# Low parts of every fourth weight piece made by an accumulating DMA instead of VectorE, in a two-layer float32 encoder trunk

## The chip, the cores and the metric

The kernel runs on one core of one Trainium2 chip. The metric is device time in microseconds (us) from the start to the end of the program. The kernel before was timed twice: 2804.89 and 2805.33 us, median 2805.11 us.

## The reference

Two layers of a bidirectional encoder on 256 tokens of width 2048, all in float32. Each layer projects the input, runs two kinds of attention, merges them through gates, and ends in a SwiGLU block; both halves are closed by a residual and a layer norm.

```python
def hybrid_layer(x, rel_bias, w_in, sink, w_pa, w_pb, w_out, ln1_g, ln1_b, w_up, w_down, ln2_g, ln2_b):
    proj = jnp.einsum('bsd,dc->bsc', x, w_in)
    qa, ka, va, qb, kb, vb, ga, gb = jnp.split(proj, split_points, axis=-1)
    ya = dilated_mixture(qa, ka, va, rel_bias).astype(dt) @ w_pa
    yb = windowed_gqa(qb, kb, vb, rel_bias, sink).astype(dt) @ w_pb
    merged = jax.nn.sigmoid(ga) * ya + jax.nn.sigmoid(gb) * yb
    x = layer_norm(DEEPNORM_ALPHA * x + merged @ w_out, ln1_g, ln1_b)
    gate, up = jnp.split(x @ w_up, 2, axis=-1)
    x = layer_norm(DEEPNORM_ALPHA * x + (jax.nn.silu(gate) * up) @ w_down, ln2_g, ln2_b)
    return x
```

The weights are 503 MB in all (w_in 2048 x 10240, w_up 2048 x 11264 and w_down 5632 x 2048 in each layer are the large ones), and every weight is used once. So the kernel streams weights from DRAM and multiplies them with activations that stay on the chip.

## The kernel before

**Two parts for every weight.** A float32 product is made of products in the chip's faster float32r format. A weight is split in a high part, the value rounded to float32r, and a low part, the value minus its high part. Activations are split in the same way. A product of tiles is then three matmuls: high by high, high by low, low by high.

**Pieces.** The weights come in 960 pieces of 512 KB, each a tile `raw` of 128 partitions by 1024 float32. `piece` (line 110) appends a piece to a list when the products are declared, and `run` (line 137) walks the list: piece `m` gets its matmuls, then, where it is the last of its product, the evacuation of the accumulator (`post`), then one step of a list of background work (attention).

Each product over the model width in `gemm_w` (line 157) has four pieces; a piece of it has eight high matmuls of 512 columns (line 202) and eight low ones of 256 columns (line 171), alternating. `gemm_a` (line 219) turns the product round, with 2 or 4 k tiles in a piece and three matmuls for each (lines 215 to 217, of which 216 reads the low part).

The order of the list in each layer, numbered from 0 in layer 0: values of attention A, pieces 0 to 23; values of B 24 to 27; keys and queries of B 28 to 47; queries and keys of A 48 to 95; then the gates and merges, 96 to 183; w_out 184 to 215; w_up, first half, 216 to 311; w_down 312 to 359; w_up, second half, 360 to 439; w_down 440 to 479. Layer 1 is the same from 480 on. In the gates and merges a cycle of eleven pieces comes back: four of a gate for A, four of a gate for B, one of w_pa, two of w_pb; four cycles are 44 pieces. Everywhere else in `gemm_w` the products start at a piece number that 4 divides.

**Loading and splitting.** `split_to` (line 121) makes the two parts of a piece. It runs ahead of the matmuls: before piece `m` is multiplied, pieces up to `m + 3` have been issued to the splitting engines, and up to eight or nine ahead close to a layer norm. The high part is a copy on ScalarE (ACT) into a tile `whi` (line 128), the low part a subtraction on VectorE (DVE) into a tile `wlo` (line 129). `load_to` (line 114) issues the loads from SyncE's DMA queue (SPq, line 118), five pieces ahead of the split, into six buffers: the load of piece `s + 6` must wait until piece `s` has been read by both splitting instructions.

The parts live in a pool of 38 buffers of 512 KB (`units`) which they share with the activations.

**What sets the order.** All engines run in program order; nothing is rescheduled. So on ACT the evacuation of a product (line 281, `tmp<-acc`) stands between the copies of the pieces three ahead of the product's last one and those that come after. ACT reaches the evacuation early, waits there for the last matmul of the product, and then copies the next pieces in one burst. The GpSimd engine (POOL) does nothing but eight tiny power operations in the layer norms (`rstd`, line 401).

Of the kernel before, what the change touches and what calls it, by code (L numbers as in the profile page):

```python
# [10 lines left out]
F32 = mybir.dt.float32  # L11
F32R = mybir.dt.float32r
BF16 = mybir.dt.bfloat16
AF = mybir.ActivationFunctionType
ALU = mybir.AluOpType
# [61 lines left out]
def trunk(ctx: ExitStack, tc: tile.TileContext, x, rel_bias, w_in, sink, w_pa, w_pb, w_out,  # L77
          ln1_g, ln1_b, w_up, w_down, ln2_g, ln2_b, hot, mask, eye, out):
    nc = tc.nc
    x = x[0]  # L80
    out = out[0]
# [10 lines left out]
    def unit(shape, dt, name):  # L92
        return units.tile(shape, dt, name=name, tag="u")
# [13 lines left out]
    state = {"load": 0, "split": 0}  # L107
# [6 lines left out]
    def load_to(m):  # L114
        while state["load"] < min(m, len(pieces)):
            pc = pieces[state["load"]]
            pc["raw"] = work.tile([P, pc["kk"], pc["cc"]], F32, name="raw", tag="raw", bufs=N_RAW)
            nc.sync.dma_start(pc["raw"], pc["src"])  # L118
            state["load"] += 1

    def split_to(m):
        while state["split"] < min(m, len(pieces)):
            load_to(state["split"] + 1 + AHEAD_LOAD)
            pc = pieces[state["split"]]
            raw = pc["raw"]
            hi = unit([P, pc["kk"], pc["cc"]], F32R, "whi")
            lo = unit([P, pc["kk"], pc["cc"]], F32R, "wlo")
            nc.scalar.activation(hi, raw, AF.Copy)  # L128
            nc.vector.tensor_tensor(out=lo, in0=raw, in1=hi.bitcast(F32), op=ALU.subtract)  # L129
            pc["hi"], pc["lo"] = hi, lo  # L130
            state["split"] += 1

# [4 lines left out]
    def run():  # L137

        for m, pc in enumerate(pieces):
            ahead = min(AHEAD_SPLIT, 1 + m)  # L140
            for n in norms:
                if n - 24 <= m < n:
                    ahead = max(ahead, min(n - m + AHEAD_NORM, AHEAD_SPLIT + (m - n + 24) // 3))
            split_to(m + 1 + ahead)
            if pc["pre"]:
                pc["pre"]()
            pc["mm"](pc)
            if pc["post"]:
                pc["post"]()
            if background:  # L150
                background.pop(0)()
            pieces[m] = None
# [662 lines left out]
    for c in range(1, 4):  # L815
        load_to(2 * c - 1)
        load_x(c)
    make(0)
    split_to(1)
    make(1)  # L820
    run()
# [28 lines left out]
```

## Time and profile before

| what | value |
|---|---|
| time, median of 2 runs | 2805.11 us |
| profiled execution | 2805.18 us, span 2803.4 us from the first instruction to the last |
| PE busy | 2778.0 us, 99% of the span |
| DVE, ACT, POOL busy | 1591.9 us (57%), 1263.2 us (45%), 5.4 us (0%) |
| granted TensorE clock, mean | 0.997 |
| DMA | 532.07 MB, mean 190 GB/s |

The page lists each engine's busy time, the chain of work that ended last, and groups of instructions with what ended the idle time before them. TensorE (PE) works nearly without a gap. The other engines wait most of their idle time for it, which costs nothing. In the timeline, a row is a stretch of like instructions with its start, its length, their count, and in brackets the idle time of the engine before it and what ended that.

### The profile page before, as it was taken

How to read it: one execution, taken by the hardware profiler on the slowest of the kernel's cores; microseconds unless marked ns; L12 is line 12 of the kernel's file. 1: busy time of each engine (PE TensorE's matmuls, PEld its weight loads, DVE VectorE, ACT ScalarE, POOL GpSimd, SP SyncE). 2: the span in 40 equal slices, each digit the busy share in tenths (PEclk: the TensorE clock that was granted, in tenths of full speed). 3: DMA queues.
4: the chain of work that ended last, by engine and by line, in shares of the span. 5: the costliest groups of instructions: out<-in, count | busy, mean ns of one | idle time of the engine just before them, and what ended most of it. 6: DMA issues, size and time to landing. Idle time of an engine off the chain costs nothing.

```text
span 2803.4 us, 38529 instructions
## 1 busy us (share of the span) xinstructions
PE 2778.0 (99%) x15467; PEld 2409.8 (86%) x15467; DVE 1591.9 (57%) x1886; ACT 1263.2 (45%) x1600; POOL 5.4 (0%) x13
## 2 busy tenths in 40 slices
PE   9999999999999999999999999999999999999998
PEld 7888888889888888888888888888888888888887
DVE  4466555576655544555566655566665555455555
ACT  4354444454444443444444545444544444334451
POOL 0000000000000000000000000000000000000000
PEclk9999999999999999999999999999999999999999
DMA  8766656664655555555746665655746556556564
GB/s 236 228 181 182 184 171 193 196 208 151 212 191 185 190 202 179 180 189 190 243 143 203 182 188 166 195 186 180 237 151 194 183 188 229 180 168 192 182 210 143
DMA packets 494982, 532.07 MB, mean 190 GB/s; under 512 B 52288, under 2 KB 424000, under 8 KB 494804
## 3 DMA queue, kind: packets, MB, share of 16 engines
q1 hardware_dynamic: 493524, 527.53, 59.6%
q8 instruction: 121, 1.98, 0.3%
q10 hardware_dynamic: 1280, 2.10, 0.3%
q14 instruction: 57, 0.47, 0.1%
HBM read 522.86 MB, written 6.68 MB: 189 GB/s over the span
## 4 chain that ended last, share of the span: by engine, by line
PE 97%; DVE 1%; SPq 1%; DMA 1%; ACT 0%; issue 0%; DVEq 0%; POOL 0%; ACTq 0%; POOLq 0%
PE acc L202 44%; PE acc L171 22%; PE acc L216 9%; PE acc L217 9%; PE acc L215 9%; SPq L118 1%; PE aux L297 0%; PE aux L296 0%; PE aux L295 0%; DMA res<-in_x_dram 0%; DMA raw<-in_w_in_dram 0%; DVE xT L392 0%; PE aux L551 0%; PE aux L517 0%; PE aux L609 0%; PE aux L533 0%
## 5 line engine op out<-in xcount | busy, mean ns | idle before, releaser
L202 PE MATMUL acc<-xT,whi 128*128 128x512 f32 x4880 | 1719.5, 398 | 0.0
L171 PE MATMUL acc<-xT,wlo 128*128 128x256 f32 x4928 | 1357.1, 281 | 0.0
L129 DVE TENSOR_TENSOR wlo<-raw,whi 128x1024 fp32r<-128x1024 f32 x960 | 1126.7, 1220 | 242.6 <-ACT whi L128 235.3
L128 ACT ACTIVATE whi<-raw 128x1024 fp32r<-128x1024 f32 x960 | 965.4, 1050 | 331.1 <-DMA raw<-in_w_down_dram 129.1
L202 PEld LDWEIGHTS acc<-xT,whi 128*128 128x128 f32 x4880 | 908.8, 188 | 206.1 <-DVE xT L392 0.3
L171 PEld LDWEIGHTS acc<-xT,wlo 128*128 128x128 f32 x4928 | 931.0, 189 | 13.4
L281 ACT ACTIVATE tmp<-acc 128x512 f32<-128x512 f32 x186 | 110.9, 596 | 745.0 <-PE acc L202 744.7
L215 PE MATMUL acc<-whi,hT 128*128 128x512 f32 (+1 forms) x784 | 288.1, 367 | 0.0
L217 PE MATMUL acc<-whi,hT 128*128 128x512 f32 (+1 forms) x784 | 288.1, 367 | 0.0
L216 PE MATMUL acc<-wlo,hT 128*128 128x512 f32 (+1 forms) x784 | 288.1, 367 | 0.0
L667 DVE TENSOR_TENSOR sg<-acc,tmp 128x512 f32<-128x512 f32 x76 | 52.5, 691 | 242.5 <-ACT tmp L281 242.5
L215 PEld LDWEIGHTS acc<-whi,hT 128*128 128x128 f32 x784 | 147.9, 189 | 24.4
L216 PEld LDWEIGHTS acc<-wlo,hT 128*128 128x128 f32 x784 | 147.8, 189 | 24.4
L217 PEld LDWEIGHTS acc<-whi,hT 128*128 128x128 f32 x784 | 147.8, 189 | 24.2
L754 DVE TENSOR_TENSOR tmp<-acc,tmp 128x512 f32<-128x512 f32 x44 | 30.4, 691 | 178.5 <-ACT tmp L281 178.5
L215 PE MATMUL acc<-whi,mT 128*128 128x512 f32 (+1 forms) x320 | 111.1, 347 | 0.0
L216 PE MATMUL acc<-wlo,mT 128*128 128x512 f32 (+1 forms) x320 | 110.9, 347 | 0.0
L217 PE MATMUL acc<-whi,mT 128*128 128x512 f32 (+1 forms) x320 | 110.9, 347 | 0.0
L435 DVE SCALAR_TENSOR_TENSOR res<-res,acc 128x1024 f32<-128x1024 f32 (+2 forms) x20 | 20.2, 1008 | 156.7 <-PE acc L217 156.7
L215 PE MATMUL acc<-whi,xT 128*128 128x512 f32 (+1 forms) x256 | 95.8, 374 | 2.9 <-ACT whi L128 2.9
L216 PE MATMUL acc<-wlo,xT 128*128 128x512 f32 (+1 forms) x256 | 95.0, 371 | 3.1 <-DVE wlo L129 3.1
L217 PE MATMUL acc<-whi,xT 128*128 128x512 f32 (+1 forms) x256 | 94.4, 369 | 0.0
(137 smaller groups left out, 1626.1 us busy)
## 6 DMA issues: line engine op xcount, KB each, us to landing
raw<-in_w_up_dram SPq DMA_DIRECT2D x352, 512.0 KB, 3.8
raw<-in_w_in_dram SPq DMA_DIRECT2D x320, 512.0 KB, 4.9
raw<-in_w_down_dram SPq DMA_DIRECT2D x176, 512.0 KB, 6.0
raw<-in_w_out_dram SPq DMA_DIRECT2D x64, 512.0 KB, 5.8
raw<-in_w_pb_dram SPq DMA_DIRECT2D x32, 512.0 KB, 3.9
raw<-in_w_pa_dram SPq DMA_DIRECT2D x16, 512.0 KB, 4.8
bias<-ftab SPq DMA_DIRECT2D x96, 64.0 KB, 3.7
ftab<-fb SPq DMA_DIRECT2D x7, 640.0 KB
```

Source lines behind the costliest of these rows:

```text
L118: nc.sync.dma_start(pc["raw"], pc["src"])
L128: nc.scalar.activation(hi, raw, AF.Copy)
L129: nc.vector.tensor_tensor(out=lo, in0=raw, in1=hi.bitcast(F32), op=ALU.subtract)
L171: nc.tensor.matmul(st["acc"][:, n, 0:SEQ], lhsT=lo[:, k, n * P:(n + 1) * P], rhs=xs(4 * j + k)[:, 0, :], start=False, stop=False)
L202: nc.tensor.matmul(acc, lhsT=hi[:, k, n * P:(n + 1) * P], rhs=xs(kt).rearrange("p h t -> p (h t)"), start=first and not turn, stop=last)
L215: nc.tensor.matmul(o, lhsT=xk[:, 0, ts], rhs=hi, start=first, stop=False)
L216: nc.tensor.matmul(o, lhsT=xk[:, 0, ts], rhs=lo, start=False, stop=False)
L217: nc.tensor.matmul(o, lhsT=xk[:, 1, ts], rhs=hi, start=False, stop=last)
L281: nc.scalar.activation(tmp, acc[:, :, SEQ:2 * SEQ], AF.Copy, scale=scale)
L435: nc.vector.scalar_tensor_tensor(r, r, scale, acc, op0=ALU.mult, op1=ALU.add)
L667: nc.vector.tensor_tensor(out=dst, in0=acc[:, :, 0:SEQ], in1=tmp, op=ALU.add)
L754: nc.vector.tensor_tensor(out=tmp, in0=acc[:, :, 0:SEQ], in1=tmp, op=ALU.add)
```

## The change

For pieces 10, 14, 18 and so on to 958, 238 in all, VectorE's subtraction goes. ACT writes the negated high part into the low tile with a second copy of the raw piece at a scale of -1, and a DMA on GpSimd's queue then adds the raw piece to it in place: -high + raw is the low part.

```diff
             nc.scalar.activation(hi, raw, AF.Copy)
-            nc.vector.tensor_tensor(out=lo, in0=raw, in1=hi.bitcast(F32), op=ALU.subtract)
+            if state["split"] % 4 == 2 and state["split"] > 8:
+                nc.scalar.activation(lo, raw, AF.Copy, scale=-1.0)
+                nc.gpsimd.dma_start(lo, raw, accum_op=ALU.add)
+            else:
+                nc.vector.tensor_tensor(out=lo, in0=raw, in1=hi.bitcast(F32), op=ALU.subtract)
```

In the changed kernel lines from 130 on stand four lower in the file: 281 becomes 285, 290 becomes 294, and so on; the new copy is line 130, the accumulating DMA line 131, the subtraction line 133.

On ACT, at the end of the first merge in layer 0 (`mT` is the split of the merged activations, `sg` a gate, `tmp` an evacuated accumulator), before:

```order
L290 ACTIVATE mT<-sg 128x2x256
L128 ACTIVATE whi<-raw 128x1024 x4
L281 ACTIVATE tmp<-acc 128x512
L711 ACTIVATE sg<-sg 128x512
L128 ACTIVATE whi<-raw 128x1024 x4
```

and in the changed kernel:

```order
L294 ACTIVATE mT<-sg 128x2x256
L128 ACTIVATE whi<-raw 128x1024
L130 ACTIVATE wlo<-raw 128x1024
L128 ACTIVATE whi<-raw 128x1024 x3
L285 ACTIVATE tmp<-acc 128x512
L715 ACTIVATE sg<-sg 128x512
```

Pieces 118 to 121 are copied here; 118 gets its second copy at once, and the other three stand one copy later.

On SPq, the loads of pieces 113 to 117 (the two of w_pb in the first merge and the three behind them) go into the buffers that pieces 107 to 111 held; the names in brackets are the semaphores waited for (DMAHW are SPq's own transfers, DMASW the GpSimd queue's, Activation and DVE the engines). Before:

```order
L118 DMA raw<-in_w_pb_dram 128x4x256 [waits DMAHW2_49,DVE_49]
L118 DMA raw<-in_w_pb_dram 128x4x256 [waits DMAHW3_49,DVE_49]
L118 DMA raw<-in_w_in_dram 128x4x256 [waits DMAHW4_49,DVE_49]
L118 DMA raw<-in_w_in_dram 128x4x256 [waits DMAHW5_49,DVE_49]
L118 DMA raw<-in_w_in_dram 128x4x256 [waits DMAHW6_49,DVE_49]
```

and in the changed kernel:

```order
L118 DMA raw<-in_w_pb_dram 128x4x256 [waits DMAHW2_49,DVE_49]
L118 DMA raw<-in_w_pb_dram 128x4x256 [waits DMAHW3_49,DVE_49]
L118 DMA raw<-in_w_in_dram 128x4x256 [waits DMAHW4_49,DVE_49]
L118 DMA raw<-in_w_in_dram 128x4x256 [waits DMAHW5_49,DMASW1_49,Activation_49]
L118 DMA raw<-in_w_in_dram 128x4x256 [waits DMAHW6_49,DVE_49]
```

The load of piece 116 now waits for the accumulating DMA of piece 110 to land, as one load in four does, and the loads behind it on the queue wait with it.

On POOL, from the start of the kernel to the first layer norms, in the changed kernel (before, only the `minus_half` row and the L401 rows stand there):

```order
L815 MEMSET minus_half 128x1
L131 DMA wlo<-raw 128x1024 x53
L405 ISA
L405 TENSOR_TENSOR rstd<-rstd,minus_half 128x1 x2
L131 DMA wlo<-raw 128x1024 x66
```

POOL issues the 238 DMAs in order (53, 66, 54 and 65), and the power operations of the norms stand between them.

## Rows read from the trace of the kernel before

**Rows 1.** The page: busy time and share of each engine; clock in 40 slices.

```profile
PE 2778.0 (99%) x15467; PEld 2409.8 (86%) x15467; DVE 1591.9 (57%) x1886; ACT 1263.2 (45%) x1600; POOL 5.4 (0%) x13
...
PEclk9999999999999999999999999999999999999999
```

**Rows 2.** The page: the chain that ended last, by engine.

```profile
PE 97%; DVE 1%; SPq 1%; DMA 1%; ACT 0%; issue 0%; DVEq 0%; POOL 0%; ACTq 0%; POOLq 0%
```

**Rows 3.** The page's costliest groups: busy us, mean ns | idle before, releaser.

```profile
L202 PE MATMUL acc<-xT,whi 128*128 128x512 f32 x4880 | 1719.5, 398 | 0.0
L171 PE MATMUL acc<-xT,wlo 128*128 128x256 f32 x4928 | 1357.1, 281 | 0.0
L129 DVE TENSOR_TENSOR wlo<-raw,whi 128x1024 fp32r<-128x1024 f32 x960 | 1126.7, 1220 | 242.6 <-ACT whi L128 235.3
L128 ACT ACTIVATE whi<-raw 128x1024 fp32r<-128x1024 f32 x960 | 965.4, 1050 | 331.1 <-DMA raw<-in_w_down_dram 129.1
```

**Rows 4.** Waits of PE: us in total, times, longest us.

```profile
PE aux L370 <- DMA res<-in_x_dram: 4.6, 2, 3.1
PE acc L216 <- DVE wlo L129: 3.1, 4, 0.9
PE acc L215 <- ACT whi L128: 2.9, 2, 2.8
```

**Rows 5.** Timeline of ACT, gates and merges of layer 0, 380 to 432 us.

```profile
385.62 3.89 ACT L128 ACTIVATE whi<-raw 128x1024 fp32r<-128x1024 f32 x4
393.31 0.60 ACT L281 ACTIVATE tmp<-acc 128x512 f32<-128x512 f32 x1 [3.80 <-PE acc L202]
...
395.21 3.89 ACT L128 ACTIVATE whi<-raw 128x1024 fp32r<-128x1024 f32 x4
404.61 0.60 ACT L281 ACTIVATE tmp<-acc 128x512 f32<-128x512 f32 x1 [5.51 <-PE acc L202]
...
406.51 1.04 ACT L128 ACTIVATE whi<-raw 128x1024 fp32r<-128x1024 f32 x1
...
413.14 0.60 ACT L281 ACTIVATE tmp<-acc 128x512 f32<-128x512 f32 x1 [3.15 <-PE acc L202]
...
416.49 3.89 ACT L128 ACTIVATE whi<-raw 128x1024 fp32r<-128x1024 f32 x4
424.18 0.60 ACT L281 ACTIVATE tmp<-acc 128x512 f32<-128x512 f32 x1 [3.80 <-PE acc L202]
```

**Rows 6.** Timeline of ACT beside the attention of layer 0, 325 to 350 us.

```profile
332.58 1.05 ACT L128 ACTIVATE whi<-raw 128x1024 fp32r<-128x1024 f32 x1
...
347.16 0.60 ACT L281 ACTIVATE tmp<-acc 128x512 f32<-128x512 f32 x1
```

**Rows 7.** Timeline of ACT in w_up, 1180 to 1215 us.

```profile
1188.14 3.89 ACT L128 ACTIVATE whi<-raw 128x1024 fp32r<-128x1024 f32 x4
1196.89 0.60 ACT L281 ACTIVATE tmp<-acc 128x512 f32<-128x512 f32 x1 [4.85 <-PE acc L202]
...
1208.13 0.60 ACT L281 ACTIVATE tmp<-acc 128x512 f32<-128x512 f32 x1 [5.46 <-PE acc L202]
```

**Rows 8.** Timeline of ACT in w_down, 985 to 1030 us.

```profile
998.86 1.06 ACT L128 ACTIVATE whi<-raw 128x1024 fp32r<-128x1024 f32 x1 [1.66 <-PE acc L216]
```

**Rows 9.** Timeline of ACT near the start, 85 to 130 us.

```profile
95.36 1.06 ACT L128 ACTIVATE whi<-raw 128x1024 fp32r<-128x1024 f32 x1 [6.00 <-DMA raw<-in_w_in_dram]
```

**Rows 10.** Timeline of PE at the same place, 97.2 to 98.5 us.

```profile
97.73 0.45 PE L216 MATMUL acc<-wlo,xT 128*128 128x256 f32 x1 [0.88 <-DVE wlo L129]
```

**Rows 11.** The tile raw: issue ns min/median/max; time from issue to landing.

```profile
L118 SPq DMA_DIRECT2D raw<-in_w_in_dram x320: 367/368/5462, 2.4 to 1918.8; - x160
...
DMA to landing us min/median/max: 3.3/4.9/11.1
```

**Rows 12.** The page: the load queue's packets, MB, share of 16 engines.

```profile
q1 hardware_dynamic: 493524, 527.53, 59.6%
```

**Rows 13.** Waits of SyncE's DMA queue: us in total, times, longest us.

```profile
SPq L118 <- DVE wlo L129: 2054.7, 887, 25.4
```

## The prediction

> **What bounds the kernel now.** I read the page first, then the waits of PE, then the timeline of ACT in each stage, because what counts here is how early a low part is finished. PE is busy for 2778.0 of 2803.4 us, at full clock in every slice [rows 1], and the chain that ended last is PE for 97% [rows 2]. The low parts cost VectorE 960 x 1.220 us, but VectorE waits for ACT, not PE for VectorE [rows 3]: in the whole program PE waited 3.1 us for a low part and 2.9 us for a high one, all in a few places at the start, and 4.6 us for the input [rows 4]. So PE's 25.4 us without work bound any gain. That is 0.9%; 2% of this kernel (56 us), about what a measurement tells from no change, can't be gained.
>
> **What the change removes: nothing on the path.** 238 subtractions x 1.220 us = 290 us go from an engine that is idle for 43% of the span [rows 1, 3]. Of what remains late nothing is a low part, so I count 0.
>
> **What it adds on ACT.** 238 copies x 1.050 us = 250 us [rows 3], on an engine that has 1540 us idle [rows 1]. In most products they fall behind the burst of copies, ahead of an evacuation that waits for PE for 3 to 5 us anyway [rows 5, 7]; the copies cost nothing there. In the merges they sit inside a burst and push its later pieces back by 1.05 us, and these are needed one piece of PE time (2.8 us) later each, so that hides as well. What counts is that the copy stands in the making of its own low part.
>
> **What it adds in time until the low part is there.** Before, the low part is ready 1.22 us after the high one. Now it takes a second copy (1.05 us), a semaphore (about 0.1), and then a time L: GpSimd writes the descriptors, the DMA reads 512 KB of raw and 512 KB of the low tile, adds, writes 512 KB back and reports. No row shows a DMA from GpSimd or one that adds. The nearest rows are the weight loads, also 512 KB into the chip: from issue to landing 3.3 us at the least, 4.9 in the median, 11.1 at most [rows 11]. I keep 3.3 and 11.1 as the ends for L. For the value: the load queue spends 59.6% of 2803.4 us on 527.53 MB [rows 12], so 512 KB (0.524 MB) cost the 16 engines 1.66 us. A second stream to read should cost as much again, since in most places the DMA starts beside two or three loads that the same burst set free. That is 4.9 + 1.66 = 6.6, plus an issue somewhat longer than SyncE's 0.37 us [rows 11], about 0.4 more: L = 7.0 us, an estimate. The high part must then be finished 7.0 + 0.1 + 1.05 = 8.15 us before PE wants the low one, or PE stands.
>
> The Trainium skill, "DMA: Bandwidth & Descriptors", section on the anatomy of a DMA on the SWDGE (gpsimd) path, gives 2.0 us plus bytes over 436 GB/s; for 512 KB that is an estimate of 3.2 us, just under the shortest load, and with it the change would cost next to nothing (the third rival). Against that stands "Collectives: The Full Stack", section on the bandwidth ceiling: an adding transfer runs at half the rate of a copy, because both sources are read on one ring. By that the second stream costs a whole one, which is the 1.66 us above. No run so far shows either.
>
> **How much time there is, stage by stage.** The timeline gives the end of a copy of the high part; the evacuation's start (which waited for PE) gives the end of a product, and counting 2.8 us for each piece (a product takes 404.61 - 393.31 = 11.30 us [rows 5]) gives when PE comes to it. In a burst each copy ends 0.95 us after the one before.
>
> - Gates and merges. Piece 118 is the first of the burst at 385.62 and ends at 386.66; it is the last piece of the product that ends at 393.3, so PE wants it at 390.4: 3.7 us. Piece 122, first of the burst at 395.21, last piece of the product that ends at 404.6: 5.4 us. Piece 126 is copied at 406.51 and opens the product behind 413.1: about 5.3 us. Piece 130, second in the burst at 416.49, opens the product behind 424.1: 5.5 us [rows 5]. Late by 4.45 + 2.75 + 2.85 + 2.65 = 12.7 us, and the pattern comes four times in the program: 51 us. Read the same way, three further pieces of each cycle have about 7 us, the rest more than 8.
> - Beside attention. Piece 102 ends at 333.63; it is the third of a product that ends at 347.1, two pieces and about 1 us of attention's matmuls before that, so about 340.5: 7 us [rows 6]. Some eleven pieces a layer stand like this.
> - These 12 + 22 pieces at about 7 us are late by 1.15 each, 39 us.
> - The start. Piece 26's copy ends at 96.4 because its load came late, and PE stood 0.9 us for its low part already at 97.73 [rows 9, 10]: late by 6.8 us. Piece 30 has about 4 us (late 4). Together 11 us.
> - w_up, 88 pieces. Of the burst at 1188.14 the fourth ends at 1192.0 and is the third piece of the product that ends at 1208.1, 5.6 us before its end: 10.5 us, so 2.3 to spare [rows 7]. Nothing late.
> - w_down and w_out, some 60 pieces. ACT there waits for buffers that PE frees [rows 8]: of 38, some 20 hold activations (8 of the normed input, 12 of the gated product), so 18 hold parts of nine pieces, and the copies run about seven pieces or 19 us ahead. Nothing late.
>
> Each delay stays: the next burst waits for the evacuation, which is late too, so nothing is caught up. Sum: 51 + 39 + 11 = 101, about 100 us.
>
> **The loads behind it.** The load of piece s + 6 and those queued behind it wait for the accumulation, where before they waited for the subtraction (887 times, 2054.7 us of waiting that cost nothing [rows 13]). Even a load issued only when PE takes up piece s has six pieces, 17 us; landing, copy and subtraction take 4.9 + 1.05 + 1.22 = 7.2 of these [rows 3, 11]. I count 0; if loads then come three at once and 5 us later, it is still 0 outside the start. On average the DMA engines go from 59.6% to 59.6 + 238 x 1.66 x (1 to 2) / 2803 = 74 to 88%, not full. The eight power operations of the norms stand behind DMAs on POOL, and a DMA there behind its ACT copy; three norms are followed by matmuls that need them, so at 1 to 2 us each this could cost 5 us. I count 0 and leave it to the range.
>
> The profiled execution took 2805.18 us, the median of the runs is 2805.11: no correction. Forecast 2805 + 100 = 2905 us, slower.
>
> **Rivals.**
> 1. L is short, 4.5 to 6.1 us, so that only the gates and the start are late: at L = 5.5 (6.65 us behind the high part) the four gate pieces are late by 2.95 + 1.25 + 1.35 + 1.15 = 6.7, four times 27 us, and the start by 8: 35 us, 2840 us. For it: a median load takes 4.9. Against it: twice the reading, and the loads beside it. It ends within 2%, from L = 6.1 down (56 us).
> 2. L is 9.3 or more, and w_up turns: its 88 pieces become late all at once. At L = 10 the 16 gate pieces cost 4 x 24.7 = 99 us, the 34 others 4.15 each = 141, w_up 0.65 x 88 = 57, the start 17, and pieces around 9 to 10 us (some 15 to 20) about 2 each, 40: 354 us, 3159 us. For it: the longest load took 11.1 us, and an adding engine might be slower than a second read. Against it: the queue isn't full.
> 3. L is that of the shortest load, 3.3 us: only 118 and its three like (0.75 each) and the start (2.9) are late, 6 us, 2811 us. Against it: a load has one stream to read, and the median is 4.9. It is what the formula quoted above from the Trainium skill, "DMA: Bandwidth & Descriptors", would lead to.
> 4. The lost subtractions speed up the start, where PE waited for low parts: at most 6 us [rows 4], 2799 us. It can't, since piece 26 there is itself an accumulated one.
>
> **How the numbers follow.** Forecast (L between 6.1 and 9.3) 0.43; rival 1 0.27; rival 2 0.23; rival 3 0.06; rival 4 0.01. Slower by over 2%: 0.43 + 0.23 = 0.66; within 2%: 0.33 with rivals 1 and 3; faster by over 2%: 0.01, kept for what I overlook. The range leaves out rival 3 and the lower edge of rival 1 below, L above 10 (about one in ten) above: 2825 to 3160. The forecast's own range, L 6.1 to 9.3, is 2861 to 3060.
>
> **What would show it.** In the changed kernel PE's waits should be led by the accumulating transfer, before L171 lines, some 50 times with 1 to 4 us each, in the gates and merges above all, and none in w_up and w_down. Time from the GpSimd issue to landing should be 6 to 8 us; VectorE should fall to 1300 us busy, ACT rise to 1510, the clock stay at full. Waits in w_up, or a landing above 9 us, would make rival 2 right; a landing under 6 us rival 1. The forecast is wrong in its reasons if PE waits for high parts or for loads instead.

## The result, and the profile after

The changed kernel takes 2907.22 us in the median (2903.46 to 2910.99), the kernel before 2805.11 us: a ratio of 1.0364, 95% interval 1.0339 to 1.0389. It is slower by 102 us; the forecast was 2905 us. The total came out, but not from the places where I had put it, and the experiments below are about that. The profiled execution is the shorter of the two, 2903.46 us.

The page after, busy time, clock and the load and GpSimd queues (packets, MB, share of 16 engines), where [rows 1, 12] stood before:

```profile
PE 2806.0 (97%) x15467; PEld 2417.2 (83%) x15467; DVE 1322.5 (46%) x1648; ACT 1484.1 (51%) x1838; POOL 210.6 (7%) x251
...
PEclk9899999999999999999999999999999999999999
...
q1 hardware_dynamic: 493524, 527.53, 58.4%
q0 software_dynamic: 34272, 124.80, 22.8%
```

PE does the same 15467 matmuls. Its time without work goes from 25.4 to 2901.7 - 2806.0 = 95.7 us, and its busy time by 28.0 us; together that is the 98.3 us by which the span grew. The longer busy time is matmuls that took longer, part of them at the lower clock (mean granted clock 0.990, before 0.997): after some of its waits PE ran at 1.2 GHz for some us. The matmuls in these stretches are busy about 12 us longer than the same matmuls before; the other 16 us are not explained here. The stretch from 100 to 175 us shows the lower clock most.

The windows of the changed kernel, 100 to 175 us, with PE, PEld, DVE, ACT and POOL busy, then PEclk, DMA share and GB/s:

```profile
100.00:175.00 75.00, 63.94 (x373) 56.92 (x373) 30.16 (x47) 36.50 (x52) 5.17 (x6) 0.90 0.86 236
```

The chain that ended last, for [rows 2], and the waits of PE, for [rows 4]:

```profile
PE 56%; DMA 22%; issue 15%; DVE 4%; ACT 3%; SPq 1%; POOL 0%; POOLq 0%; DVEq 0%; ACTq 0%
```

```profile
PE acc L175 <- DMA wlo<-raw: 37.7, 39, 2.8
PE acc L220 <- DMA wlo<-raw: 19.5, 11, 9.3
...
PE acc L219 <- ACT whi L128: 4.9, 2, 2.5
PE acc L175 <- DVE wlo L133: 4.3, 4, 1.7
PE acc L206 <- ACT whi L128: 3.2, 2, 2.3
PE acc L220 <- DVE wlo L133: 3.1, 4, 1.0
```

PE's share of the chain falls from 97 to 56%, and the DMAs' rises from 1 to 22%. What PE waits for most is the accumulated low part: 50 times, as forecast, and 57.2 us. But it waits longer for parts made by ACT and VectorE too, 15.5 us in 12 waits against 6.0 us in 6 before. Two more views of the changed kernel give the transfer itself: the source line of the DMA (issue time in ns, then issue to landing in us), and the waits of SyncE's queue, for [rows 13]:

```profile
L131 POOL DMA_DIRECT2D wlo<-raw x238: 859/859/1015, 37.1 to 2870.2; - x119
...
DMA to landing us min/median/max: 4.5/7.7/12.1
```

```profile
SPq L118 <- DMA wlo<-raw: 1272.8, 204, 29.8
SPq L118 <- DVE wlo L133: 791.4, 431, 24.3
```

**Where the time went.** The matmuls are the same and in the same order, so each piece's first use of its low part can be found in both traces, and the lag of the one behind the other read piece by piece. It grows by 28 us in the gates and merges, by 26 us in w_up, by 34 us in the start, the values and beside attention (20 + 14), and by 10 us in w_out and w_down: 98 us. I had forecast 51 + 14 = 65 us (the sixteen short pieces and twelve at about 7 us), 0, 11 + 25 = 36 us, and 0.

One place of each kind. In the merges, ACT's timeline of the changed kernel around piece 118, which had 3.7 us before [rows 5]:

```profile
409.37 1.04 ACT L128 ACTIVATE whi<-raw 128x1024 fp32r<-128x1024 f32 x1
410.32 1.04 ACT L130 ACTIVATE wlo<-raw 128x1024 fp32r<-128x1024 f32 x1
```

and PE's and POOL's at the same place:

```profile
416.75 0.39 PE L175 MATMUL acc<-xT,wlo 128*128 128x256 f32 x1 [2.28 <-DMA wlo<-raw]
```

```profile
411.65 0.86 POOL L131 DMA_DIRECT2D wlo<-raw  x1 [17.42 <-ACT wlo L130]
```

The high copy ends at 410.4, PE gets the low part at 416.7: 6.3 us and not 8.15, and PE stands for 2.3 us. In w_up, POOL and SyncE's queue:

```profile
2212.04 0.86 POOL L131 DMA_DIRECT2D wlo<-raw  x1 [9.07 <-ACT wlo L130]
2223.54 0.86 POOL L131 DMA_DIRECT2D wlo<-raw  x1 [10.63 <-ACT wlo L130]
```

```profile
2209.57 2.03 SPq L118 DMA_DIRECT2D raw<-in_w_up_dram  x4
...
2221.69 2.02 SPq L118 DMA_DIRECT2D raw<-in_w_up_dram  x4
```

PE takes up the low part of the first of the two transfers at 2221.68, 9.6 us after its issue and with hardly a wait, and at 2221.69 four loads leave, half a microsecond apart, because the first of them had waited for that landing. 1.9 us later the next transfer is issued behind them. Before, the four loads of a burst came 1.1 us apart, at the pace of VectorE's subtractions:

```profile
1190.47 3.78 SPq L118 DMA_DIRECT2D raw<-in_w_up_dram  x4
```

Not all of w_up's 26 us is a late accumulated part. In its first pieces VectorE still scales the layer norm's rows (line 429) with parameters `gb`, which come on SyncE's queue between the weights (line 424). These parameters land 9.0 us after their issue in the median, 5.8 us before. VectorE, ACT and PE shortly before piece 235, whose low part is VectorE's own:

```profile
757.86 0.69 DVE L429 TENSOR_TENSOR res<-res,gb 128x512 f32<-128x512 f32 x1 [4.41 <-DMA gb<-in_ln_g_dram]
...
762.29 0.63 ACT L294 ACTIVATE hT<-sg 128x512 fp32r<-128x512 f32 x1 [8.51 <-DVE sg L759]
...
763.92 0.51 PE L206 MATMUL acc<-xT,whi 128*128 128x512 f32 x1 [2.29 <-ACT whi L128]
```

Before, VectorE stood here for 1.5 us, ACT for 1.7 us and PE not at all. Now ACT stands behind VectorE, and PE waits 2.3 us for a high part and then 1.7 us for a low part from VectorE. The lag grows by 6.1 us at piece 235 and by 4.6 us at the same piece of layer 1: 10.7 of the 26 us.

### The profile page after: what moved, and what is told of

It reads as the page before. It is cut to its first block, busy times and chain, and to the rows that moved or that the text cites. A ratio compares the mean times of both kernels' runs of the same rounds, so it can differ in the third digit from the quotient of the medians.

```text
span 2901.7 us, 39282 instructions
## 1 busy us (share of the span) xinstructions
PE 2806.0 (97%) x15467; PEld 2417.2 (83%) x15467; DVE 1322.5 (46%) x1648; ACT 1484.1 (51%) x1838; POOL 210.6 (7%) x251
## 3 DMA queue, kind: packets, MB, share of 16 engines
q1 hardware_dynamic: 493524, 527.53, 58.4%
q0 software_dynamic: 34272, 124.80, 22.8%
## 4 chain that ended last, share of the span: by engine, by line
PE 56%; DMA 22%; issue 15%; DVE 4%; ACT 3%; SPq 1%; POOL 0%; POOLq 0%; DVEq 0%; ACTq 0%
PE acc L206 20%; PE acc L175 11%; DMA wlo<-raw 10%; PE acc L220 8%; PE acc L221 8%; PE acc L219 8%; DMA raw<-in_w_up_dram 4%; DMA raw<-in_w_in_dram 3%; DVE wlo L133 2%; ACT whi L128 1%; DMA raw<-in_w_down_dram 1%; DMA gb<-in_ln_b_dram 1%; DMA gb<-in_ln_g_dram 1%; SPq L118 1%; ACT tmp L285 1%
## 5 line engine op out<-in xcount | busy, mean ns | idle before, releaser
L133 DVE TENSOR_TENSOR wlo<-raw,whi 128x1024 fp32r<-128x1024 f32 x722 | 853.9, 1221 | 346.2 <-ACT whi L128 343.6
L131 POOL DMA_DIRECT2D wlo<-raw x238 | 205.2, 862 | 2599.5 <-ACT wlo L130 2369.3
L130 ACT ACTIVATE wlo<-raw 128x1024 fp32r<-128x1024 f32 x238 | 248.6, 1044 | 0.0
L219 PE MATMUL acc<-whi,xT 128*128 128x512 f32 (+1 forms) x256 | 96.9, 378 | 5.0 <-ACT whi L128 4.9
```

Source lines behind the costliest of these rows:

```text
L130: nc.scalar.activation(lo, raw, AF.Copy, scale=-1.0)
L131: nc.gpsimd.dma_start(lo, raw, accum_op=ALU.add)
L219: nc.tensor.matmul(o, lhsT=xk[:, 0, ts], rhs=hi, start=first, stop=False)
```

## Experiments

Each was timed in three rounds beside the kernel before on the same chip. Theory A is the prediction's: PE stands because the accumulating transfer lands too late, and nothing else costs.

**1. The second ACT copy without the DMA.**

```diff
-                nc.gpsimd.dma_start(lo, raw, accum_op=ALU.add)
+                nc.vector.tensor_tensor(out=lo, in0=raw, in1=lo.bitcast(F32), op=ALU.add)
```

> Only the second ACT copy is kept: for the 238 pieces VectorE adds the raw piece to the negated copy, no DMA. Theory A (PE stands because the accumulating transfer lands too late): the low part is ready about 2.3 us after the high one, so nothing is late outside the start; 2805 to 2812 us, no wait of PE for a low part beyond the start. Rival B (the extra copy on ACT, by its place in the bursts, delays high parts and evacuations): most of the 102 us stays, 2880 us or more.

2805.17 us, ratio 1.0001 (0.9992 to 1.0010). The extra 238 copies cost nothing, nor does the changed order on ACT. The loss belongs to the transfer.

**2. The split four pieces ahead**, and its control on the kernel before.

```diff
-AHEAD_SPLIT = 3
+AHEAD_SPLIT = 4
```

> The changed kernel with the split one piece further ahead (4 instead of 3), which gives each low part about 2.8 us more. Theory A: the waits in the gates, where the profile after shows 5 us from the negated copy to landing against 3.7 to 5.5 us of time, vanish; those beside attention too; in w_up most of them; left are the start and some of w_up: 2820 to 2845 us. Rival C (the added traffic on the DMA engines and the clock set the time, not the lateness): it stays at 2890 us or more.

> Control: the kernel before with the split four pieces ahead. All theories: PE was waiting for nothing, 2800 to 2810 us; if it is slower, part of the 41 us that stayed with four ahead belongs to that edit and not to the transfers.

2845.83 us, ratio 1.0148 (1.0132 to 1.0163), against 2803.27 us, ratio 0.9990 (0.9980 to 0.9999), for the control. 2.8 us more time per piece take away 61 of the 102 us with the same traffic on the DMA engines, so lateness, not traffic, costs; C falls. By the lag of the pieces the gates lose 0.1 us now and w_up 11, nearly all of it at piece 238 of both layers, behind a wait of VectorE for the parameters again (5 us in each); the start and attention still lose 29. The landing did not change:

```profile
wlo<-raw POOLq DMA_DIRECT2D x238, 512.0 KB, 7.6
```

The time is just above the 2820 to 2845 us expected. The control is the only version faster than the kernel before, by 0.1%, at the edge of what the runs can tell.

**3. A copying instead of an adding DMA.**

```diff
-                nc.gpsimd.dma_start(lo, raw, accum_op=ALU.add)
+                nc.gpsimd.dma_start(lo, raw)
```

> The DMA copies the raw piece over the low tile instead of adding it, so the low part of these 238 pieces is the whole value: the second read is left out, all else stays. Theory A with the second read as a main part of the landing time: packets take about 165 instead of 328 ns, the transfer 1.4 instead of 2.8 us of the engines, the landing falls from 7.7 us to about 6, and the loss to about half: 2845 to 2865 us. Rival D (the software issue and the loads queued in front are the time, the read itself is not): landing falls by under 1 us and the time stays above 2885 us.

2825.47 us, ratio 1.0070 (1.0053 to 1.0087): a fifth of the loss is left, less than I expected. The page's queue row, and the DMA's source line, of this kernel:

```profile
q0 software_dynamic: 34272, 124.80, 12.7%
```

```profile
L131 POOL DMA_DIRECT2D wlo<-raw x238: 527/527/689, 37.1 to 2790.1; - x119
...
DMA to landing us min/median/max: 2.9/6.5/9.8
```

A copy takes 0.127 x 2823.8 / 238 = 1.51 us of all 16 engines, the addition 0.228 x 2901.7 / 238 = 2.78 us. The shortest landing falls from 4.5 to 2.9 us, the median only from 7.7 to 6.5, since the loads in front remain. The second read is 1.3 us of engine time, and the issue on POOL 0.33 us more. The loss fell by more than in proportion, which fits pieces that had mostly been late by little: PE waits for 8 of these transfers instead of 50.

**4. One stage at a time.** The condition on the piece number is narrowed, for instance to w_up:

```diff
-            if state["split"] % 4 == 2 and state["split"] > 8:
+            if state["split"] % 4 == 2 and (216 <= state["split"] % 480 < 312 or 360 <= state["split"] % 480 < 440):
```

> Accumulated low parts in w_up alone (88 of the 238 pieces), VectorE elsewhere. The prediction's step (10.5 us of time against 8.15, nothing late): 2805 us. The trace after shows 28 us lost in w_up, with landings of 9 us or more behind four loads: if that is made there and not carried over from other stages, 2825 to 2835 us.

> Gates and merges alone, 44 pieces. The prediction's step (8.15 us from the high copy's end to landing) makes 51 us for the sixteen short ones and 13 us for twelve at about 7 us: 2869 us. The trace after shows 5.9 us for pieces that are copied first in their burst, and 28 us lost in these stages: 2833 us if that is made there.

> w_out and w_down alone, 60 pieces, where the copies run 15 to 20 us ahead. Theory A (only lateness costs): 2805 to 2810 us, with landings of about 7 us. Rival C (traffic or the load queue's wait costs in every stage): in proportion to the pieces, 60 of 238, 2830 us.

w_up alone 2835.63 us, ratio 1.0108 (1.0093 to 1.0123); gates and merges alone 2838.68 us, 1.0109 (1.0092 to 1.0126); w_out and w_down alone 2814.30 us, 1.0030 (1.0018 to 1.0042). Each is lost in its own stage: 30, 33 and 9 us, which with the 34 us of the start and attention make 106, near the whole 102. So w_up, which I held to be safe, costs as much as the gates, which cost half of what I had forecast, and w_down isn't free. Of w_up's 30 us, 10 are lost at piece 235 of both layers, as in the changed kernel. The landings of w_up alone and, below, of the gates alone differ by 3.4 us, and the longer one belongs to the pieces that have more time:

```profile
wlo<-raw POOLq DMA_DIRECT2D x88, 512.0 KB, 9.4
```

```profile
wlo<-raw POOLq DMA_DIRECT2D x44, 512.0 KB, 6.0
```

In w_out and w_down PE waits for the transfer six times, 6.7 us. These pieces stand within the first 20 us of their stage, where ACT has not yet run ahead; I had taken the 19 us of the middle for all of it.

**5. Another place in the burst.** Is the long landing in w_up a matter of the queue in front? The edits of this experiment and the next are shown against the kernel with w_up alone.

```diff
-            if state["split"] % 4 == 2 and (216 <= state["split"] % 480 < 312 or 360 <= state["split"] % 480 < 440):
+            if state["split"] % 4 == 0 and (216 <= state["split"] % 480 < 312 or 360 <= state["split"] % 480 < 440):
```

> w_up alone, as the run with 88 pieces there, but the piece chosen is the second of each burst of copies instead of the fourth. It has less time before PE wants it (6.8 us from the end of its high copy instead of 10.5), but its transfer is issued when only about one load of the burst is queued. Theory Q (the landing time is set by the loads queued in front: in the trace after 4.7 us from issue to landing behind none or one, 9.0 behind four): first packet at about 1.5 us, landing about 5 us, 2805 to 2825 us. Rival F (a landing of 7 to 9 us belongs to the transfer in this stage): each of the 88 is late by 1.5 to 3.5 us more than it has, 2935 us or more.

2850.09 us, ratio 1.0157 (1.0141 to 1.0172). The landing falls from 9.4 to 6.2 us with as many pieces in the same stage:

```profile
DMA to landing us min/median/max: 5.3/6.2/9.2
```

F falls: it asked for 2935 us. The time is nevertheless 25 us above my expectation, because these pieces have 6.8 - 1.35 = 5.5 us left after the second copy and the way to POOL, and the landing takes 6.2; PE waited 41 times. 17 of the 45 us are lost at pieces 235 and 236 of both layers. Sorting the transfers of the changed kernel and of six of the experiments (2, the three of 4, 5 and 6) by the number of loads issued in the 6 us before them (from the issues on both queues and the landings in the traces) gives:

| loads issued in the 6 us before | transfers | issue to landing, median | middle half |
|---|---|---|---|
| 0 | 66 | 5.1 us | 4.9 to 5.6 |
| 1 | 134 | 5.9 us | 4.9 to 6.3 |
| 2 | 181 | 6.7 us | 6.1 to 7.4 |
| 3 | 256 | 8.1 us | 7.5 to 8.8 |
| 4 or more | 163 | 9.3 us | 8.3 to 9.7 |

Each load in front adds about 1 us. With 10.5 us in w_up and 1.35 us for the second copy and the start of the issue, three loads in front are in time and four are at the edge. The count is only a rough measure, though: within the run of w_up alone it sorts nothing (9.7, 9.2 and 9.5 us behind two, three, and four or more). What SyncE's queue has issued and the DMA engines have not yet moved sorts the same 800 transfers better (correlation with the landing 0.84, against 0.71 for the count): 5.0 us behind nothing, 6.2 us behind the bytes of 1 to 1.5 loads, 8.1 behind 2 to 2.5, and 9.6 behind three or more. So what is in front is what is still under way.

**6. Half of the transfers in w_up.** Do the transfers make each other late?

```diff
-            if state["split"] % 4 == 2 and (216 <= state["split"] % 480 < 312 or 360 <= state["split"] % 480 < 440):
+            if state["split"] % 8 == 2 and (216 <= state["split"] % 480 < 312 or 360 <= state["split"] % 480 < 440):
```

> w_up alone, the fourth of every second burst, 44 pieces. Theory L (a loop: the landing of one transfer releases the load queue, its four loads go out just ahead of the next transfer and make that one late): with a burst between, the loads have drained, at most three loads stand in front, landings of 7 to 8 us, nothing late: 2805 to 2812 us. Rival (each transfer costs by itself): half of the 30 us, 2820 us.

2810.77 us, ratio 1.0017 (1.0008 to 1.0027): half of the transfers cost 5 us, not 15. Of the 5 us, 3.7 are lost at piece 235 of layer 0, and PE waits for a transfer only once, 1.0 us. With a burst in between, the loads are back at VectorE's pace and three stand in front of the transfer (SyncE's queue, then POOL, then the landing, of this kernel):

```profile
1206.02 2.64 SPq L118 DMA_DIRECT2D raw<-in_w_up_dram  x3
```

```profile
1208.82 0.86 POOL L131 DMA_DIRECT2D wlo<-raw  x1 [21.74 <-ACT wlo L130]
```

```profile
DMA to landing us min/median/max: 4.6/8.1/10.5
```

**7. The blocked loads on GpSimd's own queue**, with w_up alone (shown without the condition of experiment 4), and with the split four ahead for all 238 pieces (there without the limits on the stage).

```diff
+            old = state["load"] - N_RAW
-            nc.sync.dma_start(pc["raw"], pc["src"])
+            (nc.gpsimd if old % 4 == 2 and (216 <= old % 480 < 312 or 360 <= old % 480 < 440) else nc.sync).dma_start(pc["raw"], pc["src"])
```

> w_up alone with all 88 pieces, but the loads into buffers that an accumulated piece held go on GpSimd's queue, so SyncE's loads no longer wait for a landing and no longer leave four at a time. Theory L (the loop through the load queue): at most three loads stand in front of a transfer, it lands in about 8 us, 9.3 us after the high copy's end against 10.5: 2806 to 2815 us. Rival (the loads of the same burst alone make it late, the wait on SyncE's queue does not matter): 2830 to 2840 us as without this edit.

> All 238 pieces, split four ahead, and the loads behind accumulated pieces on GpSimd's queue: both remedies together. Theory: of the 41 us that stayed with four ahead the 11 us in w_up go, and some of the 18 us beside attention; left are the start and attention, 2820 to 2835 us. If it were to reach 2803 us (the kernel before with four ahead) the idea would be free; I do not expect that.

w_up alone: 2845.90 us, ratio 1.0141 (1.0126 to 1.0157), slower than without the edit. My expectation was wrong, and POOL's timeline shows why:

```profile
1193.38 0.77 POOL L119 DMA_DIRECT2D raw<-in_w_up_dram  x1 [9.26 <-DVE wlo L134]
1194.13 0.89 POOL L132 DMA_DIRECT2D wlo<-raw  x1
```

The load no longer holds up SyncE's queue, but now it is issued directly in front of the next transfer on the same queue, and SyncE's three come beside it: still four in front, and the median landing stays at 9.4 us. The edit moved the load and did not take it out of the way. It also gave the transfers a new wait: 24 of the 88 are issued more than half a microsecond after their second copy, 20 us in all, most of it behind a load that stands waiting on GpSimd's queue; with w_up alone that is 1 of 88. So it fits the loads in front as the cause and not SyncE's wait as the whole loop, but it is no clean test of either. With four ahead and all pieces the time is 2837.82 us, ratio 1.0118 (1.0103 to 1.0133), a gain of some 8 us over four ahead alone, at the edge of what the runs can tell, and outside the 2820 to 2835 us expected.

## Why the prediction was right, and where not

**Nothing is gained on the path, and the ACT copy is free.** Both hold: VectorE lost 269 us of work and ACT gained 221 us, and experiment 1 is at 1.0001.

**PE stands for the accumulated low part, and each delay stays.** It holds for most of the time: 50 waits, 1.1 us in the mean and up to 9.3 us, and more time per piece (experiment 2) takes most of the loss away without changing traffic or landing. DMA engines were used for 58.4 + 22.8 = 81% on these two queues, inside the 74 to 88% expected, so traffic as such does not bound. The waits are not where they were forecast, above all in the gates and merges and none in w_up: both have 18.

**The second read.** The prediction added 1.66 us of engine time for it; experiment 3 has 2.78 against 1.51 us, 1.27 us more. "Collectives: The Full Stack" of the Trainium skill, section on the bandwidth ceiling, has the adding step of a ring collective at half the rate of a copying one, because two sources are read on one ring; 2.78 / 1.51 = 1.84 is near that. "DMA: Bandwidth & Descriptors" of the Trainium skill, section on the anatomy of a DMA on the SWDGE (gpsimd) path, has 2.0 us plus bytes over 436 GB/s, an estimate of 3.2 us for 512 KB; the shortest copy (2.9 us) is near it, the shortest addition (4.5 us) is not. No addition landed in the 3.3 us of the third rival.

**L = 7.0 us was one number for all stages, and this step failed.** "In most places the DMA starts beside two or three loads" is true of the median (7.7 us from the issue), but where there is little time the transfer is the first of its burst and runs nearly alone (4.6 to 6.7 us for the sixteen short pieces), and where there is much it is the last and runs behind four loads (9.4 us). The gates and merges, 65 us in the sum, cost 33 alone; w_up, 0 in the sum, costs 30. In the changed kernel the gates were put 37 us too high, w_up and w_out with w_down 26 and 10 us too low, and the start and attention came to 34 for 36 only because 20 + 14 stood in place of 11 + 25. That these errors cancel and 2905 and 2907 us agree is chance. The gates behave as in rival 1, which has 27 us for their sixteen short pieces at L = 5.5. Rival 2 was in part right: w_up does turn, but as landings hover around the 9.3 us that I gave as its point, PE waits for only 18 of the 88 pieces, 12.5 us in all. The 0.1 us for the semaphore stood in no row; POOL starts 0.29 us after the second copy ends.

**"The loads behind it: I count 0" failed as well.** I had asked whether the loads would come too late for ACT; they do not. What I missed is what they run into when the landing sets them free: the next transfer. I also had only weight loads in view: the layer norm's parameters come on the same queue, and their lateness takes 10.7 of w_up's 26 us by way of VectorE and ACT. In experiment 7 SyncE's loads wait for no landing, and piece 235 still costs 5.7 and 5.4 us, so that wait is not needed for it. Experiment 6 speaks for transfers that make each other late, and the timeline of the changed kernel has the four loads leaving at the landing. Which part of the fourth load's delay is SyncE's wait and which its mere place in front was not separated, since experiment 7 kept four in front.

**w_out and w_down, 0 in the sum, cost 9 us** at their beginnings. The reading of one row in the middle was carried to the edges.

**The clock** was said to stay full. It fell to 1.2 GHz in short stretches after some waits, and those are in the 28 us of longer busy time, with about 12 us when the same matmuls of both traces are compared. No run tried this by itself.

## What to carry to other kernels

Moving work off an engine that nobody waits for gains nothing, and the replacement must be priced by the time from its start to its landing against the time until it is wanted, piece by piece, not by its mean share of an engine. A transfer's landing time is set by what was issued in front of it: the place of an issue within a burst of loads was worth more here (5.1 us behind nothing, 9.4 us behind a burst) than its own cost (2.8 us). And when a transfer holds a buffer, ask what leaves at the moment when it lands, what that will be in front of, and what else comes on the queue that waits.

## What was not expected of the hardware

- A DMA issued on GpSimd's queue started later, the more load data issued earlier on SyncE's was still under way. From the packets in the trace of the changed kernel, the first packet of an accumulation comes 1.4 us after the issue with no or one load in front and 5.0 us after with four. The section on queues and rings in "DMA: Bandwidth & Descriptors" of the Trainium skill says that a DMA engine takes turns between queues packet by packet; by that the first packet should come soon after the issue with any number of loads in front. The traces here do not show that, and why is open.
- The issue on GpSimd takes 0.86 us for the adding and 0.53 us for the copying DMA of the same 512 KB, against 0.37 us on SyncE's queue [rows 11].
- A wait of PE of about 2 us was followed by the lower clock in some places and not in others: after 2.0 us of waiting before 1872.6 the granted clock was 0.51 (1.2 GHz), after 2.3 us before 416.75 it stayed at 1.00. So a PE that stands can pay a second time.
